# w_gu with four rows of a partition side by side, loaded by halves of an expert

## The chip, the cores and the metric

The kernel runs on one core of a Trainium2 chip. The metric is the device time of one execution in microseconds. Before the change the median of three runs is 1074.6 us (1073.11 to 1078.62).

## The reference

One decoder layer on 256 tokens of width 1024, all in float32. A state-space mixer (S5 with a GLU) and a cross-attention into 256 memory rows read one input projection; their outputs are joined by w_out, added to the input and normalized. What the change touches is the mixture of experts that follows:

```python
logits = xt @ router_w + router_b
top_val, top_idx = lax.top_k(logits, 4)          # of 32 experts
gates = softmax(top_val)
# for every expert e, on the tokens that chose it:
gu = xb @ w_gu[e] + b_gu[e]                      # 1024 -> 2048
x_glu = minimum(gu[..., :1024], 7.0)
x_lin = clip(gu[..., 1024:], -7.0, 7.0)
act = x_glu * sigmoid(1.702 * x_glu) * (x_lin + 1.0)
y = act @ w_down[e] + b_down[e]                  # 1024 -> 1024
out = sum over the chosen experts of gate * y
```

followed by a second residual and layer norm. Each expert's w_gu is 1024 x 2048 floats (8 MB) and its w_down 1024 x 1024 (4 MB); the 32 experts together are 402.7 million bytes, and every one is read once.

## The kernel before, in words

SBUF holds one tile `big` of 23 slots; a slot is 2048 floats on each of 128 partitions, 1 MB. The mixer's phase (until about 143 us) keeps its tensors in these slots under names (`slot_of`, L85 to L92; `big_tile`, L94). Slots 0 to 21 form eleven blocks of two neighbouring slots, 2 MB each, and they are also the ring through which the experts' weights stream: `ring` (L99) holds the blocks' first slots in the order in which the mixer's phase lets go of them, and `next_block` (L101) takes the first and puts it behind the last.

`load_gu` (L1183) issues four loads for an expert's w_gu, one for each block. A load has 256 rows of w_gu, two to a partition: partition p gets rows 2p and 2p + 1, which lie next to each other in HBM, so each partition's part is one run of 16 KB. `load_down` (L1192) issues two loads for w_down, four rows of 4 KB to a partition, also runs of 16 KB. The loads are issued on SyncE (SP), whose instructions are kept in the order in which they are written (`Ordered`, L127). A load waits, on SyncE, until the matmuls that read the block's former content are done; later loads stand behind it. Six loads make an expert. At e = 18 one block leaves the ring for b_down and the last norm's rows (L1302 to L1307), and ten remain.

On TensorE, expert after expert: `up` (L1113) multiplies the expert's gathered tokens (64 slots, transposed) with w_gu in eight steps of 128 rows; `act` runs on VectorE and ScalarE; meanwhile TensorE gathers the tokens of the next two experts (`gather_pair`, L1084, at odd e) or adds the finished pair of experts into the output's accumulators (`combine`, L1159, at even e); then `act_t` transposes the activations, `up_bias` starts the next expert's sums with its bias, and `down` (L1145) multiplies with w_down. A step of 128 rows of w_gu takes every second row of a load (row t * 256 + 2 * r + j for step 2t + j), so the gather picks the columns of h_sb in the same order through `hv` (L1058), with a step of two floats between neighbouring columns.

The last two experts are arranged by hand (L1309 to L1348): expert 31's w_gu is loaded before expert 30's w_down, and expert 31's w_down in smaller cuts. A branch for experts with more than 64 tokens (L1382 on) uses the same functions; the times below are without it.

Of the kernel before, what the change touches and what calls it, by code (L numbers as in the profile page):

```python
# [16 lines left out]
P = 128  # L17
D = 1024
NT = 256
KT = D // P  # L20
# [3 lines left out]
NE = 32  # L24
# [2 lines left out]
LN_EPS = 1e-5  # L27
MISS = 8192.0
ROWS = 2
NBIG = 23  # L30

LOG2E = 1.4426950408889634
# [9 lines left out]
def kernel(  # L42
# [32 lines left out]
    V, S, PE, G, SP = nc.vector, nc.scalar, nc.tensor, nc.gpsimd, nc.sync  # L75

    keep = ctx.enter_context(tc.tile_pool(name="keep", bufs=1))
    big = ctx.enter_context(tc.tile_pool(name="big", bufs=1)).tile([P, NBIG * 2048], F32, tag="big", name="big")
    psum = ctx.enter_context(tc.tile_pool(name="psum", bufs=8, space=bass.MemoryType.PSUM))
# [2 lines left out]
    prep = pre.enter_context(tc.tile_pool(name="pre", bufs=1))  # L82


    slot_of = {}  # L85
    for k, names in enumerate((
# [3 lines left out]
    )):  # L90
        for name in names.split():
            slot_of[name] = k  # L92

    def big_tile(name):  # L94
        k = slot_of[name]
        return big[:, 2048 * k : 2048 * (k + 1)]


    ring = [2 * k + n for k in (0, 1, 2, 3, 4, 8, 6, 10, 7, 9, 5) for n in range(0, 2, ROWS)]  # L99

    def next_block():  # L101
        ring.append(ring.pop(0))
        return big[:, 2048 * ring[-1] : 2048 * (ring[-1] + ROWS)]

    def bank(name):
        return psum.tile([P, 512], F32, tag="ps", name=name)
# [32 lines left out]
    SP = Ordered(SP)  # L139

    def mm(o, lhsT, rhs, start, stop, shared=False):
        pin(PE.matmul(o, lhsT, rhs, start=start, stop=stop, skip_group_check=shared))  # L142
# [7 lines left out]
    def ts(o, x0, s1, op0, s2=None, op1=ALU.bypass, eng=None):  # L150
        return (eng or V).tensor_scalar(out=o, in0=x0, scalar1=s1, scalar2=s2, op0=op0, op1=op1)
# [34 lines left out]
    for k2 in range(4):  # L186
        t = big_tile(f"win_{k2}").rearrange("p (k n) -> p k n", k=2)
        rows = w_in[2 * k2 * P : (2 * k2 + 2) * P, :].rearrange("(k p) n -> p k n", p=P)
# [390 lines left out]
    for b in range(3):  # L579
        ps = bank(f"kb{b}")  # L580
# [59 lines left out]
    for b in range(3):  # L640
        for a in range(2):
            ps = bank(f"kc{b}{a}")
# [66 lines left out]
    for r2 in range(3):  # L709
        ps = bank(f"sip{r2}")  # L710
# [14 lines left out]
    for q in range(2):  # L725
        dst = sv[q].rearrange("p (j l c) -> p l j c", j=4, l=6)
        for l0, l1 in ((0, 4), (4, 6)):
            ps = bank(f"stp{q}{l0}")
# [62 lines left out]
    for i in range(2):  # L791
        for m in range(2):
            ps = bank(f"pTp{i}{m}")
# [71 lines left out]
    for t4 in range(2):  # L865
        ts_ = slice(4 * t4, 4 * t4 + 4)
        ps = bank(f"yTa{t4}")
# [3 lines left out]
    for t4 in range(2):  # L871
        ts_ = slice(4 * t4, 4 * t4 + 4)
        ps = bank(f"yTb{t4}")
# [10 lines left out]
    for mq in range(6):  # L884
        ps = bank(f"zp{mq}")
# [45 lines left out]
    h_sb = big_tile("h_sb").rearrange("p (i d) -> p i d", i=2)  # L931
# [21 lines left out]
    def wt(shape, tag, name, dt=F32):  # L953
        n = 2 if tag == "ogT" else 1
        return work.tile(list(shape), dt, tag=tag, name=f"{tag}_{name}", bufs=n)
# [54 lines left out]
    def up_bias(n, sel, ps=None):  # L1010

        ps = [bank(f"gu{b}_{n}") for b in range(2)] if ps is None else ps
        for hf in range(2):
            for b in range(2):
                mm(
                    ps[b][64 * hf : 64 * hf + 64, :], sel[2 * b + hf],
                    bgu[NE * (2 * b + hf) : NE * (2 * b + hf) + NE, :], True, False, True,
                )
        return ps

    def sel_of(e):
        return [ident[NE * q : NE * q + NE, NE * q + e : NE * q + e + 1].to_broadcast([NE, CAP]) for q in range(4)]
# [25 lines left out]
    ps = up_bias("e0", sel_of(0))  # L1048
# [6 lines left out]

    dbg("@experts", None)

    hv = h_sb.rearrange("p i (t r j) -> p i t j r", r=P, j=ROWS)  # L1058

    def gather(n, xg, ranks, base, between=lambda: None, after=lambda: None, oh=None):  # L1060

        w = CAP * len(ranks)
        first_too = oh is None
        oh = wt((P, 2, 2 * CAP), "oh", n) if oh is None else oh
        ps = [bank(f"xgp{k}_{n}") for k in range(len(ranks))]
        for i in range(2):
            if i:
                between()
            for k, rank in enumerate(ranks):
                if i or first_too:  # L1070
                    ts(oh[:, i, CAP * k : CAP * k + CAP], base, rank[i], ALU.is_equal)
            if i:
                after()
            for kt in range(KT):
                c = w * kt % 512
                mm(
                    ps[w * kt // 512][:, c : c + w], hv[:, i, kt // ROWS, kt % ROWS], oh[:, i, 0:w],
                    c == 0 and i == 0, i == 1, True,
                )
        k = 512 // w  # L1080
        for n_, p in enumerate(ps):
            S.copy(xg[:, k * n_ : k * n_ + k, :], p.rearrange("p (k c) -> p k c", k=k))

    def gather_pair(n, xg, ranks):  # L1084

        oh = wt((P, 2, 2 * CAP), "oh", n)
        for i in range(2):
            for k, rank in enumerate(ranks):
                ts(oh[:, i, CAP * k : CAP * k + CAP], iota64, rank[i], ALU.is_equal)
        for k4 in range(2):  # L1090
            ps = bank(f"xgp{k4}_{n}")
            for i in range(2):
                for kt in range(4 * k4, 4 * k4 + 4):
                    mm(
                        ps[:, P * (kt % 4) : P * (kt % 4) + P], hv[:, i, kt // ROWS, kt % ROWS], oh[:, i, :],
                        kt % 4 == 0 and i == 0, i == 1, True,
                    )
            S.copy(xg[:, 4 * k4 : 4 * k4 + 4, :], ps.rearrange("p (k c) -> p k c", k=4))
# [36 lines left out]
    def act_t(n, a, ps=None, at=None):  # L1135
        ps = bank(f"atp_{n}") if ps is None else ps
        av = a.rearrange("s (c p j) -> s c j p", p=P, j=2 * ROWS)
        for c in range(4):
# [41 lines left out]
                mm(ps, ogT[:, i, :], y[:, ds_], True, True)  # L1180
                tt(acc[:, i, ds_], acc[:, i, ds_], ps, ALU.add)

    def load_gu(src):  # L1183

        w = []
        for t in range(KT // ROWS):
            b = next_block().rearrange("p (j n) -> p j n", j=ROWS)
            SP.dma_start(b, src[t * ROWS * P : (t + 1) * ROWS * P, :].rearrange("(p j) n -> p j n", j=ROWS))
            w += [b[:, j, :] for j in range(ROWS)]
        return w  # L1190

    def load_down(src, split=False):  # L1192
# [50 lines left out]
    def load_gb2(n):  # L1243
        return padded("rows2", D, ((slice(0, 1), ln2_g), (slice(1, 2), ln2_b)))
# [56 lines left out]
    for e in range(NE):  # L1301
        if e == NE - 14:  # L1302
            k = ring[0]
            slot_of.update(bd=k, gb2=k, rows2=k + 1, o=k + 1)
            del ring[0 : 2 // ROWS]
            late = padded("bd", D + NT, ((slice(0, NE), b_down[0]),))
            rows2 = load_gb2("e")  # L1307
        gu = load_gu(w_gu[0, e]) if e < NE - 1 else gu_last
        if e == NE - 2:  # L1309
            gu_last = load_gu(w_gu[0, e + 1])  # L1310
        if e != NE - 2:
# [20 lines left out]
        if e == NE - 2:  # L1332
# [6 lines left out]
            ps = up_bias(f"e{e + 1}", sel_of(e + 1), tb[1:3])  # L1339
# [26 lines left out]
        ps = up_bias(f"e{e + 1}", sel_of(e + 1))  # L1366
# [15 lines left out]
    with tc.If(fullest > CAP):  # L1382
# [6 lines left out]
        with tc.For_i(0, NE, 1) as e:  # L1389
# [10 lines left out]
            for rnd in range(1, NT // CAP):  # L1400
# [10 lines left out]
                ps = up_bias(f"f{rnd}", sel)  # L1411
                gu = load_gu(gsrc)
# [45 lines left out]
```

## Time and profile before

| | |
|---|---|
| median of 3 runs | 1074.6 us (1073.11 to 1078.62) |
| the profiled execution's own time | 1072.42 us |
| its span, first to last instruction | 1070.6 us |
| TensorE matmul busy | 1003.3 us, 94% |
| mean granted TensorE clock | 0.995 |
| bytes moved by DMA | 424.61 MB, 397 GB/s over the span |

The profile is that of one execution. PE is TensorE, PEld its weight loads, DVE is VectorE, ACT ScalarE, POOL GpSimd, and SPq the instructions of SyncE's sequencer, among them the issues of loads. A matmul's end is modelled, so a busy TensorE is not one at its peak. Most instructions carry the line of a helper (L142 is `mm`, L145 `tr`, L135 the ordered engines); they are told apart by the names of what they write and read.

### The profile page before, as it was taken

How to read it: one execution, taken by the hardware profiler on the slowest of the kernel's cores; microseconds unless marked ns; L12 is line 12 of the kernel's file. 1: busy time of each engine (PE TensorE's matmuls, PEld its weight loads, DVE VectorE, ACT ScalarE, POOL GpSimd, SP SyncE). 2: the span in 40 equal slices, each digit the busy share in tenths (PEclk: the TensorE clock that was granted, in tenths of full speed). 3: DMA queues.
4: the chain of work that ended last, by engine and by line, in shares of the span. 5: the costliest groups of instructions: out<-in, count | busy, mean ns of one | idle time of the engine just before them, and what ended most of it. 6: DMA issues, size and time to landing. Idle time of an engine off the chain costs nothing.

```text
span 1070.6 us, 12357 instructions
## 1 busy us (share of the span) xinstructions
PE 1003.3 (94%) x5297; PEld 442.6 (41%) x5297; DVE 245.6 (23%) x531; ACT 150.4 (14%) x288; POOL 49.2 (5%) x90
## 2 busy tenths in 40 slices
PE   9999999999999999999999988899999999898994
PEld 8886554434343434343434332323333343333331
DVE  7984251111111111111111111110111111111113
ACT  3494020101010101010101000000101110100001
POOL 5810000000000000000000000000000000000001
PEclk9999999999999999999999999999999999999998
DMA  9949989999999999999999999999999999999992
GB/s 303 166 151 329 424 314 429 428 417 430 427 428 427 425 429 428 426 430 427 428 426 429 429 409 428 429 428 427 427 427 428 427 428 427 427 428 428 429 422 98
DMA packets 43939, 424.61 MB, mean 397 GB/s; under 512 B 11251, under 2 KB 14215, under 8 KB 19177
## 3 DMA queue, kind: packets, MB, share of 16 engines
q1 hardware_dynamic: 43384, 422.73, 95.9%
q10 hardware_dynamic: 496, 1.05, 0.3%
q8 instruction: 43, 0.70, 0.3%
q14 instruction: 16, 0.12, 0.0%
HBM read 421.93 MB, written 1.84 MB: 396 GB/s over the span
## 4 chain that ended last, share of the span: by engine, by line
PE 50%; DMA 45%; DVE 2%; ACT 1%; issue 0%; SPq 0%; ACTq 0%; POOL 0%; DVEq 0%; POOLq 0%
DMA big<-in_exp_w_gu_dram 29%; PE gu_e L142 20%; PE dn_e L142 11%; DMA big<-in_exp_w_down_dram 11%; PE xgp_e L142 4%; DMA big<-in_exp_b_down_dram 4%; PE accp L142 3%; PE yp L142 3%; DVE big L135 2%; PE ups L142 1%; PE zp L142 1%; DMA big<-in_l_w_in_dram 1%; PE tail L142 1%; ACT big L135 1%; PE atp_e L145 1%; PE qps L142 1%
## 5 line engine op out<-in xcount | busy, mean ns | idle before, releaser
L142 PE MATMUL gu_e<-big,xg_e 128*64 128x512 f32 x1984 | 439.8, 594 | 44.2 <-DMA big<-in_exp_w_gu_dram 43.5
L142 PEld LDWEIGHTS gu_e<-big,xg_e 128*64 128x64 f32 x1984 | 138.3, 137 | 340.0 <-issue 253.0
L142 PE MATMUL dn_e<-big,xl_te 128*64 128x512 f32 x960 | 212.6, 595 | 0.0
L142 PEld LDWEIGHTS dn_e<-big,xl_te 128*64 128x64 f32 x960 | 66.3, 137 | 144.3 <-issue 119.6
L1127 DVE TENSOR_SCALAR xl_e<-gu_e 128x512 f32<-128x512 f32 x31 | 21.4, 691 | 429.2 <-PE gu_e L142 429.2
L1155 DVE COPY y_e<-dn_e 64x512 f32<-64x512 f32 x30 | 20.5, 684 | 265.7 <-PE dn_e L142 265.7
L135 ACT ACTIVATE gu_e<-xl_e 128x512 f32<-128x512 f32 x31 | 18.6, 601 | 403.7 <-DVE xl_e L1127 403.7
L142 PEld LDWEIGHTS xgp_e<-oh_e,big 128*128 128x128 f32 x544 | 65.4, 196 | 13.3 <-PE gu_e L142 12.2
L142 PE MATMUL xgp_e<-oh_e,big 128*128 128x128 f32 (+1 forms) x544 | 68.7, 284 | 0.0
L142 PE MATMUL accp<-y_e,ogT_e 128*128 128x512 f32 x128 | 59.4, 603 | 0.8 <-DVE y_e L1155 0.8
L135 ACT COPY y_e<-dn_e 64x512 f32<-64x512 f32 x30 | 17.5, 582 | 244.0 <-DVE y_e L1155 244.0
L142 PEld LDWEIGHTS accp<-y_e,ogT_e 128*128 128x128 f32 x128 | 23.2, 190 | 35.3 <-issue 33.7
L142 PE MATMUL gu_e<-bgu,ident 32*64 32x512 f32 x248 | 34.3, 612 | 0.0
L135 DVE TENSOR_TENSOR big<-big 128x96 f32<-128x96 f32 (+8 forms) x47 | 29.0, 635 | 21.1 <-ACT big L135 16.2
L142 PE MATMUL yp<-big 128*128 128x512 f32 x64 | 28.6, 596 | 0.0
L135 DVE TENSOR_TENSOR big<-big,tab 128x2048 f32<-128x2048 f32 x12 | 26.5, 2276 | 0.2 <-DVE big L135 0.2
L135 ACT COPY xl_te<-atp_e 128x512 f32<-128x512 f32 x30 | 17.9, 595 | 60.4 <-PE atp_e L145 57.5
L135 ACT COPY xg_e<-xgp_e 128x512 f32<-128x512 f32 x32 | 18.8, 587 | 53.4 <-PE xgp_e L142 53.4
L1131 DVE TENSOR_TENSOR xr_e<-xr_e,gu_e 128x512 f32<-128x512 f32 x31 | 21.3, 687 | 6.4 <-ACT gu_e L135 3.3
L135 POOL TENSOR_TENSOR yv<-yv,mhalf 128x1 f32<-128x1 f32 x2 | 1.1, 550 | 468.9 <-DVE yv L135 468.9
L1238 POOL MEMSET big<- 128x1280 f32 (+1 forms) x2 | 2.1, 1058 | 447.0 <-PE gu_e L142 447.0
L1130 DVE SCALAR_TENSOR_TENSOR xr_e<-xr_e,xl_e 128x512 f32<-128x512 f32 x32 | 22.1, 692 | 1.1
(289 smaller groups left out, 586.7 us busy)
## 6 DMA issues: line engine op xcount, KB each, us to landing
big<-in_exp_w_gu_dram SPq DMA_DIRECT2D x128, 2048.0 KB, 39.1
big<-in_exp_w_down_dram SPq DMA_DIRECT2D x62, 2048.0 KB, 33.8
big<-in_l_w_in_dram SPq DMA_DIRECT2D x3, 1024.0 KB
big<-in_w_out_dram SPq DMA_DIRECT2D x3, 1024.0 KB, 9.2
big<-in_exp_w_down_dram SPq DMA_DIRECT2D x3, 1024.0 KB
big<-in_x_dram SPq DMA_DIRECT2D x3, 512.0 KB, 3.5
big<-in_l_s_w_glu_dram SPq DMA_DIRECT2D x2, 768.0 KB
big<-in_l_w_in_dram SPq DMA_DIRECT2D x2, 512.0 KB, 6.8
```

The costliest lines, as they stand in the source:

```text
L135: return lambda *a, **k: pin(f(*a, **k))
L142: pin(PE.matmul(o, lhsT, rhs, start=start, stop=stop, skip_group_check=shared))
L145: pin(PE.transpose(o, in_, ident if idn is None else idn))
L1127: V.tensor_scalar(out=xl_, in0=ps[0], scalar1=7.0, scalar2=None, op0=ALU.min)
L1130: V.scalar_tensor_tensor(out=xr, in0=xr, scalar=1.0, in1=xl_, op0=ALU.add, op1=ALU.mult)
L1131: a = V.tensor_tensor(out=xr, in0=xr, in1=sg, op=ALU.mult)
L1155: eng(y[:, 512 * dh : 512 * dh + 512], ps[dh][64 * dh : 64 * dh + 64, :])
L1238: G.memset(t[:, 0:width], 0.0)
```

## The change

The slots are renumbered so that the ring's order is 0, 2, 4 up to 20: a name that stood in block b now stands in the block at b's place in the old order. `load_gu` takes 512 rows at a time, four to a partition, so that a partition's part is one run of 32 KB over two blocks. For experts 3 to 28, and where the two blocks are neighbours in memory, both are filled by one load of 4 MB; otherwise each block is filled by a load of its own, with the first or the second 16 KB of each run. The steps of `up` and the gather follow with `GJ = 4`: step 4t + j takes row t * 512 + 4 * r + j, and neighbouring columns of h_sb are four floats apart.

```diff
--- before.py
+++ after.py
@@ -27,6 +27,7 @@
 LN_EPS = 1e-5
 MISS = 8192.0
 ROWS = 2
+GJ = 4
 NBIG = 23
 
 LOG2E = 1.4426950408889634
@@ -82,6 +83,7 @@
     prep = pre.enter_context(tc.tile_pool(name="pre", bufs=1))
 
 
+    free_order = (0, 1, 2, 3, 4, 8, 6, 10, 7, 9, 5)
     slot_of = {}
     for k, names in enumerate((
         "ptmp0 wsc", "ptmp1 gt", "m20", "m21", "m22", "u_sb", "cab s_in tw yg", "memT xs", "bbt tz0", "bab att",
@@ -89,14 +91,14 @@
         "win_3 wgl0", "win_0 sv wo2", "win_1 tz2 ymT", "wk wgl1", "pow yT", "wv h_sb",
     )):
         for name in names.split():
-            slot_of[name] = k
+            slot_of[name] = 2 * free_order.index(k // 2) + k % 2 if k < 22 else k
 
     def big_tile(name):
         k = slot_of[name]
         return big[:, 2048 * k : 2048 * (k + 1)]
 
 
-    ring = [2 * k + n for k in (0, 1, 2, 3, 4, 8, 6, 10, 7, 9, 5) for n in range(0, 2, ROWS)]
+    ring = list(range(0, 22, ROWS))
 
     def next_block():
         ring.append(ring.pop(0))
@@ -1055,7 +1057,7 @@
 
     dbg("@experts", None)
 
-    hv = h_sb.rearrange("p i (t r j) -> p i t j r", r=P, j=ROWS)
+    hv = h_sb.rearrange("p i (t r j) -> p i t j r", r=P, j=GJ)
 
     def gather(n, xg, ranks, base, between=lambda: None, after=lambda: None, oh=None):
 
@@ -1074,7 +1076,7 @@
             for kt in range(KT):
                 c = w * kt % 512
                 mm(
-                    ps[w * kt // 512][:, c : c + w], hv[:, i, kt // ROWS, kt % ROWS], oh[:, i, 0:w],
+                    ps[w * kt // 512][:, c : c + w], hv[:, i, kt // GJ, kt % GJ], oh[:, i, 0:w],
                     c == 0 and i == 0, i == 1, True,
                 )
         k = 512 // w
@@ -1092,7 +1094,7 @@
             for i in range(2):
                 for kt in range(4 * k4, 4 * k4 + 4):
                     mm(
-                        ps[:, P * (kt % 4) : P * (kt % 4) + P], hv[:, i, kt // ROWS, kt % ROWS], oh[:, i, :],
+                        ps[:, P * (kt % 4) : P * (kt % 4) + P], hv[:, i, kt // GJ, kt % GJ], oh[:, i, :],
                         kt % 4 == 0 and i == 0, i == 1, True,
                     )
             S.copy(xg[:, 4 * k4 : 4 * k4 + 4, :], ps.rearrange("p (k c) -> p k c", k=4))
@@ -1180,13 +1182,22 @@
                 mm(ps, ogT[:, i, :], y[:, ds_], True, True)
                 tt(acc[:, i, ds_], acc[:, i, ds_], ps, ALU.add)
 
-    def load_gu(src):
+    def load_gu(src, whole=False):
 
         w = []
-        for t in range(KT // ROWS):
-            b = next_block().rearrange("p (j n) -> p j n", j=ROWS)
-            SP.dma_start(b, src[t * ROWS * P : (t + 1) * ROWS * P, :].rearrange("(p j) n -> p j n", j=ROWS))
-            w += [b[:, j, :] for j in range(ROWS)]
+        for t in range(KT // GJ):
+            rows = src[t * GJ * P : (t + 1) * GJ * P, :].rearrange("(p j) n -> p j n", j=GJ)
+            next_block(), next_block()
+            k0, k1 = ring[-2:]
+            if whole and k1 == k0 + ROWS:
+                b = big[:, 2048 * k0 : 2048 * (k0 + GJ)].rearrange("p (j n) -> p j n", j=GJ)
+                SP.dma_start(b, rows)
+                w += [b[:, j, :] for j in range(GJ)]
+                continue
+            for n, k in enumerate((k0, k1)):
+                b = big[:, 2048 * k : 2048 * (k + ROWS)].rearrange("p (j n) -> p j n", j=ROWS)
+                SP.dma_start(b, rows[:, ROWS * n : ROWS * n + ROWS])
+                w += [b[:, j, :] for j in range(ROWS)]
         return w
 
     def load_down(src, split=False):
@@ -1305,7 +1316,7 @@
             del ring[0 : 2 // ROWS]
             late = padded("bd", D + NT, ((slice(0, NE), b_down[0]),))
             rows2 = load_gb2("e")
-        gu = load_gu(w_gu[0, e]) if e < NE - 1 else gu_last
+        gu = load_gu(w_gu[0, e], 3 <= e < NE - 3) if e < NE - 1 else gu_last
         if e == NE - 2:
             gu_last = load_gu(w_gu[0, e + 1])
         if e != NE - 2:
```

## Rows read from the trace of the kernel before

**Rows 1.** The page's second part: 40 equal slices of the span, busy tenths, then GB/s.

```profile
PE   9999999999999999999999988899999999898994
...
DMA  9949989999999999999999999999999999999992
GB/s 303 166 151 329 424 314 429 428 417 430 427 428 427 425 429 428 426 430 427 428 426 429 429 409 428 429 428 427 427 427 428 427 428 427 427 428 428 429 422 98
```

**Rows 2.** Chain of waits: start us, us, what; two experts, then the hops.

```profile
255.83 7.02 PE dn_e L142 x32
...
281.69 7.08 PE dn_e L142 x32
...
308.22 7.02 PE dn_e L142 x32
...
484.44 39.09 DMA big<-in_exp_w_gu_dram
...
1002.92 39.09 DMA big<-in_exp_w_down_dram
```

**Rows 3.** Windows: stretch, length, busy us (x instructions) by engine, PEclk, DMA share, GB/s.

```profile
135.80:139.00 3.20, 3.20 (x11) 1.69 (x11) 2.42 (x10) 0.00 (x0) 0.00 (x0) 1.00 0.00 0
139.00:229.60 90.60, 87.18 (x456) 40.20 (x456) 22.54 (x62) 11.45 (x21) 0.55 (x1) 0.98 1.00 417
229.60:234.60 5.00, 5.00 (x26) 1.69 (x24) 0.00 (x0) 0.00 (x0) 0.00 (x0) 1.00 1.04 416
234.60:240.00 5.40, 5.40 (x28) 1.75 (x26) 0.68 (x1) 0.58 (x1) 0.00 (x0) 1.00 0.94 388
240.00:440.00 200.00, 200.00 (x990) 79.55 (x988) 33.42 (x71) 18.98 (x35) 0.00 (x0) 1.00 1.01 428
```

**Rows 4.** The same view over stretches with 1 KB and 4 KB runs.

```profile
34.00:38.00 4.00, 4.00 (x25) 3.64 (x24) 4.00 (x3) 2.49 (x5) 4.00 (x2) 1.00 1.04 366
76.00:80.00 4.00, 4.00 (x51) 3.36 (x53) 3.93 (x7) 3.92 (x10) 0.19 (x1) 1.00 1.01 393
78.00:80.00 2.00, 2.00 (x42) 1.59 (x44) 1.93 (x3) 1.94 (x4) 0.19 (x1) 1.00 1.03 412
```

**Rows 5.** SyncE's timeline: start us, us from first to last, queue, line, what, xcount.

```profile
138.06 0.33 SPq L135 DMA_DIRECT2D big<-in_exp_w_gu_dram  x1
...
183.33 3.76 SPq L135 DMA_DIRECT2D big<-in_exp_w_gu_dram  x2
...
199.46 0.33 SPq L135 DMA_DIRECT2D big<-in_exp_w_gu_dram  x1
...
209.76 3.76 SPq L135 DMA_DIRECT2D big<-in_exp_w_gu_dram  x2
...
216.63 0.33 SPq L135 DMA_DIRECT2D big<-in_exp_w_gu_dram  x1
...
232.98 0.33 SPq L135 DMA_DIRECT2D big<-in_exp_w_gu_dram  x1
...
236.41 3.76 SPq L135 DMA_DIRECT2D big<-in_exp_w_down_dram  x2
...
285.38 0.33 SPq L135 DMA_DIRECT2D big<-in_exp_w_gu_dram  x1
```

**Rows 6.** TensorE's timeline; in brackets the idle time before, and its cause.

```profile
219.04 5.40 PE L142 MATMUL accp<-big,xl_alpha 128*128 128x512 f32 x8 [2.45 <-DVE xl_alpha L1163]
...
229.28 7.09 PE L142 MATMUL dn_e<-big,xl_te 128*64 128x512 f32 x32
...
622.96 3.65 PE L142 MATMUL gu_e<-big,xg_e 128*64 128x512 f32 x16 [2.76 <-DMA big<-in_exp_w_gu_dram]
627.86 2.37 PE L142 MATMUL gu_e<-big,xg_e 128*64 128x512 f32 x10 [1.25 <-DMA big<-in_exp_w_gu_dram]
```

**Rows 7.** TensorE's weight loads, 240 to 440 us: xcount, busy us, mean ns, idle before.

```profile
L142 PEld LDWEIGHTS xgp_e<-oh_e,big 128*128 128x128 f32 x128 | 15.4, 196 | 3.2 <-PE gu_e L142 3.2
...
L145 PEld LDWEIGHTS atp_e<-ident,xr_e 128*128 128x128 f32 x32 | 4.8, 205 | 1.9 <-issue 1.9
```

## The prediction

> **What bounds the kernel now.** I read the busy shares by slice first, then the chain of waits, the windows by stage, and SyncE's own timeline. The slices show TensorE and the DMA engines both near full, so neither is the bound by its share alone [rows 1]. The chain separates them in time: until about 446 us it runs through TensorE, expert after expert, and after that it jumps from one weight load to the next in hops of 39.09 us down to the last at 1002.92, which lands at 1042.01; a short tail on TensorE follows [rows 2]. Two consecutive experts take 308.22 - 255.83 = 52.39 us of TensorE, 26.2 us each. A hop of 39.09 us is eight loads (SyncE issues a load when the eighth before it has landed), 4.89 us for 2 MB, so six loads of an expert take 29.3 us. TensorE is therefore 3.1 us per expert faster than the queue. It starts with a full ring, eats that lead up by 446 us, and from then on follows the queue.
>
> So the end is set by the DMA queue over the whole stretch from 139 us on. Nothing moves from 135.8 to 139.0; after that the engines' share stays at 1.0, from 240 us on with 428 GB/s, and only at 234.6 to 240.0 does it dip, to 0.94 and 388 GB/s [rows 1, 3]. Any microsecond in which the queue has nothing to do between 139 and 1040 us, early or late, arrives at the end whole; any gain in rate does too, as long as TensorE keeps some of its 3.1 us. That dip is the place to look at: the queue was all but empty there.
>
> **The change, part by part.** Numbering loads from 0, six per expert, load n goes into the block of load n - 11 until expert 18, where the ring drops to ten blocks.
>
> *The number of whole pairs.* Between e = 3 and 28 there are 26 x 2 = 52 pairs. A pair that straddles the ring's end stays two loads: e = 5, 9, 16 (one each) with eleven blocks, e = 18, 21, 23, 26, 28 with ten. 44 become one load of 4 MB.
>
> *Longer contiguous runs.* A load is 128 runs, eight per DMA engine. The trace has no 32 KB run, so I take the cost of a run from the rates: 16 KB runs at 428 GB/s take 16384 / (428/16) = 612.5 ns on an engine; the 4 KB runs of w_out, at 412 GB/s from 78 to 80 us, take 159.1 ns [rows 4]. That is (612.5 - 159.1) / 12288 = 0.0369 ns a byte, and 159.1 - 4096 x 0.0369 = 8.0 ns are left as a constant of each run. A whole pair has eight runs fewer on each engine: 8 x 8.0 = 64 ns, 0.064 us. The wider window at 393 GB/s, which takes in loads of smaller runs, would give 18 ns a run and 0.146 us; the 1 KB runs at 366 GB/s give 6.9 ns [rows 4]. The lower end is zero: a long run may still be moved in 16 KB pieces. I take 0.064 us, since 4 KB is the nearest clean row: over 40 pairs -2.6 us, ends 0 and -5.8. (40, not 44: what the first four pairs save only lengthens the stall below.)
> The Trainium skill, "DMA: Bandwidth & Descriptors", section "Why small descriptors are slow (HBM only)", speaks of a fixed overhead of some 3 cycles a packet, with beats of 32 bytes. By that rule two 16 KB runs are 1030 beats and one 32 KB run 1027, an estimate of 0.029 us a pair and -1.1 us in all, which would make the sum +3.4 instead of +1.9; the rows show a larger constant, and I go by them.
>
> *The wait that is added.* A whole pair may be issued only when both of its blocks are free, that is when its second load was issued before. While TensorE sets the pace, a load is issued the moment its block is read out: 3.43 us apart inside w_gu, with a break of 9 to 16 us where combine, transposes and bias lie. Going through the early pairs against the queue [rows 3, 5]: 139.0 to 229.6 us at 417 GB/s is 37.8 MB, exactly the 18 loads 8 to 25, so load 25 is done at about 229.6.
> - Expert 3, loads 18/19: issue 186.76 instead of 183.33 (the row's 3.76 us less the 0.33 of one issue); load 17 ends at about 190.3, covered. Loads 20/21: 199.46 for both, where the first of them went out 9 us earlier; load 19 ends at about 200.1, and with the cold start below the queue loses about 1 us, which the next item swallows.
> - Expert 4, loads 24/25: 213.19 instead of 209.76, with the queue busy to about 220; covered. Loads 26/27: before, 26 was issued at 216.63, and its transfer (229.6 to 234.6) is what kept the queue alive until 27 was issued at 232.98. Now neither goes out before 232.98, when TensorE is halfway through the w_down matmuls of expert 2 (229.28 to 236.37 [rows 6]). The queue is dry from about 230.
> - What a cold start costs: the load issued at 138.06 moves its first byte at 139.0, 0.95 us later; and load 27, issued at 232.98, was done at 240.0, 7.0 us for 4.89 us of data, 2.1 us [rows 3, 5]. With 1.8 us as the value, the pair is done at 232.98 + 1.8 + 9.7 = 244.5 instead of 240.0: +4.5 us; with 0.95 +3.6, with 2.1 +4.8.
> Behind the waiting load on SyncE stand the w_down loads of expert 4, which were issued at 236.41 anyway because their blocks come free then; they lose nothing more. For expert 6, loads 38/39 wait to 285.38, while the queue, now 4.5 us late, is busy with loads 28 to 37 until 244.5 + 10 x 4.89 = 293.4. From there the margin grows by 3.1 us an expert; after 446 us the ring's eleven blocks are 54 us of queue time (ten: 49), a load is read out within some 20 us of landing, and a pair is free about 30 us before its turn. One stall, then.
>
> *Halves of an expert for TensorE.* Before 446 us it works on data that landed long ago. After that it waits for 4 MB where it waited for 2 MB: two waits of about 1.25 us per expert [rows 6] become one of about 3 us. The total is the 3.1 us that it has to spare, so this costs nothing; a wait of 2.76 us at 622.96 left the clock alone, while 2.45 us at 219.04 preceded the one stretch at half clock, which the windows show as 0.98 up to 229.6 [rows 3, 6]. Should each long wait cost such a drop, TensorE would have some 1.7 us more per expert and still fit. The last three experts are loaded as before, so the tail is what it was.
>
> *The rest at nothing.* The gather reads h_sb at a step of four floats instead of two: its weight loads take 196 ns on average, the transposes that already step by four 205 ns [rows 7], at most 9 ns x 64 before 232.98, +0.6 us. Renumbering moves tiles within `big` and leaves the order of reuse as it was. Half as many load issues on SyncE: 0.33 us each, hidden behind a 39 us backlog. The halves of experts 0 to 2, 29 to 31 and of split pairs have 16 KB runs as now, 32 KB apart.
>
> **Sum.** +4.5 - 2.6 = +1.9 us, ends -2.2 (3.6 - 5.8) and +5.4 (4.8 + 0.6, nothing saved). On the profiled execution's own 1072.42 us (span 1070.6 and 1.8 around it) that is 1074.3. The median of the runs shown stands 2.2 us above that execution, so I predict 1074.6 + 1.9 = 1076.5 us.
>
> **Rivals.**
> - *No stall, only the shorter transfers.* If the queue is restarted in the shadow of bytes still under way, or the blocks come free sooner, 44 pairs at 0.064 give 1074.6 - 2.8 = 1071.8, and at 0.146 1068.2. The rows for the dip at 234.6 speak against it: with load 26 in front, load 27 came just too late.
> - *The runs stay 16 KB inside the engines.* Then only the stall is left: 1074.6 + 4.5 = 1079.1. The steady constant from 1 KB to 16 KB speaks for a cost per run, but nothing shows a longer run.
> - *Slower: rows 32 KB apart are read more slowly.* Every w_gu load changes its reach: an engine's neighbours start twice as far apart in HBM. Place: all w_gu loads from expert 3 on, 29 x 19.6 = 568 us of queue time, so each per cent of rate is 5.7 us; from 0.6% on it carries my +1.9 past half a per cent of the kernel (5.4 us), and at 2% it gives 1076.5 + 11.4 = 1087.9. Against it: w_out with 4 KB rows and w_gu with 16 KB rows lie on one line of cost per byte. The Trainium skill, same page, section "Latency and other measured facts", tells of copies that slow down with a large power-of-two row pitch: 207 GB/s of 214 at 512 KiB, 103 at 4 MiB. By that rule 32 KB would lie well below where the loss begins, and the case would give 1076.5 again; no row here has a pitch above 16 KB, so the case keeps its chance.
>
> **How the numbers follow.** Forecast 0.62, no stall 0.14, runs stay short 0.12, slower reads 0.12. A difference under 0.5% (5.4 us: 1069.2 to 1080.0) can't be told from none. Faster: half of the no-stall case and a little of the forecast, 0.08. Slower: most of the slow reads and a share of the third and the first, 0.16. Within: 0.76. The range runs from the middle of the no-stall case, 1070, to the stall with no saving and the spread of the runs (1073.1 to 1078.6) on top, 1082.
>
> **What would show it.** Right: the page lists some 44 loads of 4096 KB; a window with almost no bytes between 230 and 235 us; then a rate a little above 428 GB/s, 430 or so. Wrong: no empty window near 232 (the stall), a rate still at 427 to 428 (the runs), a rate below it (slow reads), or SyncE waiting for TensorE after 446 us with the engines' share below 1.0, which would mean that the ring, not the queue, sets the pace.

## The result, and the profile after

The changed kernel takes 1087.14 us (median of 4 runs, 1085.90 to 1090.71) against 1074.56 us of the kernel before in the same comparison (4 runs, 1073.11 to 1078.62): a ratio of 1.0128, 95% interval 1.0106 to 1.0151. That is 12.6 us slower, where 1.9 us and no difference that can be told were forecast. The profiled execution is the longest of the four, 1090.71 us with a span of 1089.0.

The page of the changed kernel: granted clock and GB/s in 40 slices, the sums of the chain, the whole pairs (count, size, median us from issue to landing), and the gather's weight loads from the costliest groups.

```profile
PEclk9999968999999999999999999999999999999998
...
GB/s 298 173 128 327 425 235 318 377 385 394 426 429 428 431 430 433 430 428 431 427 431 429 427 423 416 430 431 428 435 429 429 429 430 431 421 429 429 426 423 115
...
PE 89%; DMA 7%; DVE 2%; ACT 1%; issue 0%; ACTq 0%; POOL 0%; DVEq 0%; POOLq 0%
...
L144 PEld LDWEIGHTS xgp_e<-oh_e,big 128*128 128x128 f32 x544 | 128.3, 329 | 13.7 <-PE gu_e L144 12.2
...
big<-in_exp_w_gu_dram SPq DMA_DIRECT2D x44, 4096.0 KB, 31.4
```

The 44 whole pairs are there. Against [rows 1], slices 6 to 10 (136 to 272 us) move 235 to 394 GB/s where they moved 314 to 430; from slice 11 on the rate is about as before, in most slices a little above it. The clock's row, which on the page of before has a 9 in every slice but the last, has a 6 and an 8 in slices 6 and 7. So the time went between 136 and 252 us, in a stretch where the forecast had the queue covered but for one dip. On the costliest list the gather has changed: its weight loads take 329 ns where [rows 7] has 196, and its matmuls grow with them (the row is shown further down).

TensorE's timeline of the changed kernel, first three gathers (start us, us from first to last, instructions; in brackets the idle time before):

```profile
147.05 4.00 PE L144 MATMUL xgp_e<-oh_e,big 128*128 128x64 f32 x16
...
152.23 3.81 PE L144 MATMUL xgp_e<-oh_e,big 128*128 128x64 f32 x16
156.77 16.89 PE L144 MATMUL gu_e<-big,xg_e 128*64 128x512 f32 x64 [0.73 <-ACT xg_e L137]
...
173.80 7.73 PE L144 MATMUL xgp_e<-oh_e,big 128*128 128x64 f32 x32
...
184.23 8.25 PE L144 MATMUL dn_e<-big,xl_te 128*64 128x512 f32 x32
...
206.14 7.73 PE L144 MATMUL xgp_e<-oh_e,big 128*128 128x128 f32 x32
```

The same stretch of the kernel before:

```profile
149.80 13.95 PE L142 MATMUL gu_e<-big,xg_e 128*64 128x512 f32 x64 [0.73 <-ACT xg_e L135]
163.89 3.98 PE L142 MATMUL xgp_e<-oh_e,big 128*128 128x64 f32 x32
...
169.33 7.09 PE L142 MATMUL dn_e<-big,xl_te 128*64 128x512 f32 x32
```

A gather of 32 matmuls takes 7.73 us instead of 3.98. The two matmul groups behind slow gathers took longer as well, 16.89 for 13.95 us and 8.25 for 7.09, though the change does not touch them. The w_down matmuls of expert 0 start at 184.23 instead of 169.33, 14.9 us late. Of that 2.3 us are older than any gather: in this execution the router's first matmuls begin at 136.59 instead of 134.32. (Among the profiled executions of both layouts this start lies anywhere between 134.32 and 136.59.) The gathers give 7.4 us (4.00 + 3.81 against twice 2.10 for the first, 7.73 against 3.98 for the second). Most of the rest goes with two stretches at half clock, which the windows show (columns as in [rows 3]); first the changed kernel:

```profile
130.00:252.00 122.00, 118.62 (x520) 60.06 (x520) 29.93 (x80) 12.64 (x23) 1.61 (x2) 0.89 0.81 332
145.60:162.80 17.20, 16.47 (x62) 10.56 (x56) 6.33 (x26) 3.64 (x7) 0.00 (x0) 0.50 0.70 275
159.90:164.30 4.40, 4.40 (x16) 1.27 (x14) 1.04 (x5) 0.00 (x0) 0.00 (x0) 0.68 0.00 0
176.40:186.60 10.20, 10.20 (x40) 6.65 (x42) 0.74 (x4) 1.17 (x2) 0.00 (x0) 0.50 0.82 349
186.30:189.90 3.60, 3.60 (x18) 1.12 (x16) 0.00 (x0) 0.00 (x0) 0.00 (x0) 0.96 0.00 0
216.70:220.10 3.40, 3.40 (x18) 1.15 (x16) 0.00 (x0) 0.00 (x0) 0.00 (x0) 1.00 0.00 0
252.00:1000.00 748.00, 746.11 (x3422) 323.40 (x3420) 111.54 (x235) 66.62 (x123) 2.05 (x2) 1.00 1.00 428
```

and the kernel before:

```profile
130.00:252.00 122.00, 118.58 (x605) 54.29 (x604) 32.55 (x84) 13.80 (x25) 1.62 (x2) 0.99 0.96 400
...
252.00:1000.00 748.00, 706.94 (x3440) 273.36 (x3440) 112.38 (x240) 68.02 (x126) 2.05 (x2) 1.00 1.01 427
```

SyncE's timeline of the changed kernel at the three stretches with 0 GB/s:

```profile
163.41 0.33 SPq L137 DMA_DIRECT2D big<-in_exp_w_down_dram  x1
...
189.09 0.33 SPq L137 DMA_DIRECT2D big<-in_exp_w_gu_dram  x1
...
219.21 0.33 SPq L137 DMA_DIRECT2D big<-in_exp_w_gu_dram  x1
```

The reader is to see three things. The queue stands still three times, at 159.9, 186.3 and 216.7: each time SyncE issues the next load only at 163.41, 189.09 and 219.21, and of the 125 us that it waits between 130 and 252 us, 115 are for TensorE's matmuls, those that still read the blocks above all. From 145.6 to 162.8 and from 176.4 to 186.6 the granted clock is 0.50, that is 1.2 of 2.4 GHz; the second stretch begins 2.6 us into a slow gather, the first 1.4 us before one. And between 130 and 252 us the kernel moves (400 - 332) GB/s x 122 us = 8.3 MB less than before, 19.4 us of queue time at 428 GB/s, while from 252 to 1000 us it moves 1 GB/s more (320.40 MB against 319.37, 2.4 us). The difference, 17.0 us, and the 2.3 us of the late start are about what separates the two profiled executions (1090.71 - 1072.42 = 18.3). From 252 us on TensorE is busy for 746.11 of 748 us, and the chain follows it for 89% of the span; yet the DMA engines are full there too, as before. Which of them sets the end is not told by the chain; a run below decides it (`late32`).

### The profile page after: what moved, and what is told of

Its sections match the earlier page's. It is cut to its first block, busy times and chain, and to the rows that moved or that the text cites. A ratio compares the mean times of both kernels' runs of the same rounds, so it can differ in the third digit from the quotient of the medians.

```text
span 1089.0 us, 12257 instructions
## 1 busy us (share of the span) xinstructions
PE 1064.4 (98%) x5297; PEld 512.7 (47%) x5297; DVE 245.8 (23%) x531; ACT 150.4 (14%) x288; POOL 49.2 (5%) x90
## 4 chain that ended last, share of the span: by engine, by line
PE 89%; DMA 7%; DVE 2%; ACT 1%; issue 0%; ACTq 0%; POOL 0%; DVEq 0%; POOLq 0%
PE gu_e L144 39%; PE dn_e L144 19%; PE xgp_e L144 12%; PE accp L144 5%; DMA big<-in_exp_w_down_dram 4%; DMA big<-in_exp_w_gu_dram 3%; PE yp L144 3%; PE ups L144 2%; DVE big L137 2%; PE zp L144 1%; PE atp_e L147 1%; ACT big L137 1%; PE tail L144 1%; PE qps L144 1%; PE busy L144 1%; PE kb L144 0%
## 5 line engine op out<-in xcount | busy, mean ns | idle before, releaser
L144 PE MATMUL gu_e<-big,xg_e 128*64 128x512 f32 x1984 | 434.2, 595 | 2.6 <-DMA big<-in_exp_w_gu_dram 1.9
L144 PEld LDWEIGHTS gu_e<-big,xg_e 128*64 128x64 f32 x1984 | 142.8, 138 | 288.2 <-issue 283.1
L144 PEld LDWEIGHTS xgp_e<-oh_e,big 128*128 128x128 f32 x544 | 128.3, 329 | 13.7 <-PE gu_e L144 12.2
L144 PE MATMUL xgp_e<-oh_e,big 128*128 128x128 f32 (+1 forms) x544 | 131.5, 404 | 0.0
L153 DVE TENSOR_SCALAR oh_e<-iota,rk 128x64 f32<-128x64 f32 x62 | 12.8, 252 | 85.2 <-PE xgp_e L144 85.2
```

## The experiments

Nine kernels ran. A text on record calls the kernel before B and the changed one A. The ratios are to the kernel before in the same comparison, as recorded with it; they are not the quotients of the medians (1087.14 / 1074.56 is 1.0117 for the changed kernel, where the ratio is 1.0128). Losses in microseconds are differences of medians.

**Which part of the change costs.** Theory S: the gather's step of four floats (TensorE's weight loads) costs it. Theory P: the whole pairs, their waits or their 32 KB runs, do.

`a_step2`: the changed kernel with the gather's step of before, in both gather functions.
```
-    hv = h_sb.rearrange("p i (t r j) -> p i t j r", r=P, j=GJ)
+    hv = h_sb.rearrange("p i (t r j) -> p i t j r", r=P, j=ROWS)
...
-                    ps[w * kt // 512][:, c : c + w], hv[:, i, kt // GJ, kt % GJ], oh[:, i, 0:w],
+                    ps[w * kt // 512][:, c : c + w], hv[:, i, kt // ROWS, kt % ROWS], oh[:, i, 0:w],
```


> The changed kernel, with the gather reading h_sb at a step of two floats again (it then gathers other columns than the weights' rows, so only the times count). Theory S (the step of the gather): its 544 weight loads take 196 ns and follow each other every 118 ns again, TensorE gets 62.8 us back, the queue's early dry stretches of 4.5, 3.8 and 3.6 us at 160, 186 and 217 us are gone but for the one that whole pairs bring at expert 4, and the time is 1076 us (1073 to 1079). Theory P (the whole pairs' wait and the 32 KB runs): nothing changes in them, 1087 us.

Measured 1071.94 us against 1073.96, ratio 0.9982 (0.9964 to 1.0000): all of the loss is gone, and the median is 2.0 us below the kernel before, with an interval that reaches 1. The gather's weight loads in its groups (count, busy us, mean ns, idle before):

```profile
L144 PEld LDWEIGHTS xgp_e<-oh_e,big 128*128 128x128 f32 x544 | 65.5, 196 | 13.3 <-PE gu_e L144 12.2 <-DVE m L137 0.8 <-DVE oh_e L137 0.2
```

and its windows:

```profile
130.00:252.00 122.00, 118.58 (x615) 54.88 (x613) 32.94 (x84) 14.39 (x26) 1.62 (x2) 1.00 0.94 391
...
230.00:240.00 10.00, 10.00 (x48) 3.30 (x46) 0.68 (x1) 0.58 (x1) 0.00 (x0) 1.00 0.80 318
252.00:1000.00 748.00, 713.98 (x3435) 277.68 (x3435) 112.49 (x239) 67.59 (x126) 2.05 (x2) 0.98 1.00 429
```

`b_step4`: the kernel before with the changed kernel's step and nothing else.
```
-    hv = h_sb.rearrange("p i (t r j) -> p i t j r", r=P, j=ROWS)
+    hv = h_sb.rearrange("p i (t r j) -> p i t j r", r=P, j=4)
...
-                    ps[w * kt // 512][:, c : c + w], hv[:, i, kt // ROWS, kt % ROWS], oh[:, i, 0:w],
+                    ps[w * kt // 512][:, c : c + w], hv[:, i, kt // 4, kt % 4], oh[:, i, 0:w],
```


> The kernel before, with the gather reading h_sb at a step of four floats and nothing else changed (other columns are gathered, only the times count). Theory S: weight loads of 329 ns, 62.8 us more on TensorE, half-clock stretches between 145 and 190 us, the queue dry early, 1083 to 1088 us. Theory P: 1074.6 us, as before, with TensorE's spare time taking the longer gather.

Measured 1086.31 us, ratio 1.0136 (1.0106 to 1.0166), +12.4 us: one edit of an access pattern, no load touched, gives the whole loss. The two parts add up to 10.4 us beside the 12.6 measured, inside their intervals. S stands; P is out. Its windows show a kernel whose queue runs short early only:

```profile
130.00:252.00 122.00, 118.58 (x536) 60.18 (x536) 30.41 (x81) 12.71 (x24) 1.61 (x2) 0.94 0.88 357
...
252.00:1000.00 748.00, 747.30 (x3430) 323.76 (x3428) 110.83 (x234) 66.59 (x123) 2.05 (x2) 1.00 1.01 427
```

`a_perm`: the changed kernel with h_sb kept in the gather's order, so that the weight loads read neighbouring floats; the norm's two VectorE operations and the combine's matmul permute instead.
```
-    h_sb = big_tile("h_sb").rearrange("p (i d) -> p i d", i=2)
+    h_sb = big_tile("h_sb").rearrange("p (i t j r) -> p i t j r", i=2, j=GJ, r=P)
+
+    def by_step(half):
+        return half.rearrange("p (r j) -> p j r", j=GJ)
...
-        stt(h_sb[:, i, hs], x2[:, i, hs], mean[i], gb[:, 0, hs], ALU.subtract, ALU.mult)
+        stt(h_sb[:, i, hf], by_step(x2[:, i, hs]), mean[i], by_step(gb[:, 0, hs]), ALU.subtract, ALU.mult)
...
-        stt(h_sb[:, i, hs], h_sb[:, i, hs], rs[i], gb[:, 1, hs], ALU.mult, ALU.add)
+        stt(h_sb[:, i, hf], h_sb[:, i, hf], rs[i], by_step(gb[:, 1, hs]), ALU.mult, ALU.add)
...
-    hv = h_sb.rearrange("p i (t r j) -> p i t j r", r=P, j=GJ)
+    hv = h_sb
...
-                    mm(accp[i][hf], alpha_id, h_sb[:, i, 512 * hf : 512 * hf + 512], True, False)
+                    mm(by_step(accp[i][hf]), alpha_id, h_sb[:, i, hf], True, False)
```


> The changed kernel with h_sb stored in the order of the steps, so that the gather's weight loads read 128 neighbouring floats; the norm writes it in that order, and the first matmuls into the accumulators write their sums back in the natural one. Theory S: weight loads of 190 ns, every 118 ns or a little less, and 1073 to 1077 us; if the norm's strided reads cost VectorE something just before the first expert, up to 3 us more. Theory P: 1087 us.

Measured 1076.24 us, ratio 1.0037 (1.0021 to 1.0054), +2.3 us, and 4.3 above `a_step2`, from which only the gather, the norm and the combine's first matmuls differ. The weight loads are cured, but the norm became slower in turn. Its gather's weight loads, in the groups:

```profile
L144 PEld LDWEIGHTS xgp_e<-oh_e,big 128*128 128x128 f32 x544 | 62.6, 193 | 13.8 <-PE gu_e L144 12.2 <-DVE big L137 0.8 <-DVE oh_e L137 0.7
```

VectorE's timeline at the norm (start us, us, instructions):

```profile
132.85 2.20 DVE L137 SCALAR_TENSOR_TENSOR big<-big,mv 128x512 f32<-128x512 f32 x2
```

the same two operations of the kernel before:

```profile
132.03 1.41 DVE L135 SCALAR_TENSOR_TENSOR big<-big,mv 128x512 f32<-128x512 f32 x2
```

and two windows of `a_perm` behind them:

```profile
150.40:157.20 6.80, 6.07 (x19) 2.47 (x19) 2.70 (x11) 3.64 (x7) 0.00 (x0) 0.50 0.85 313
157.60:159.40 1.80, 1.80 (x10) 0.56 (x8) 0.00 (x0) 0.00 (x0) 0.00 (x0) 1.00 0.04 9
```

Reading two inputs at a step of four floats costs VectorE 1.10 us an operation instead of 0.70. The router's matmuls begin as in `a_step2` (135.14 and 135.16), but the matmuls with w_gu behind the first gather start 1.7 us later (152.31 and 150.65); then the clock is down for 6.8 us and the queue all but dry for 1.8. The strided read was moved to another engine and paid there; why the clock fell is not shown.

`b_step8`: the step at eight floats, to see whether the price grows with the bytes passed over.
```
-    hv = h_sb.rearrange("p i (t r j) -> p i t j r", r=P, j=ROWS)
+    hv = h_sb.rearrange("p i (t r j) -> p i t j r", r=P, j=8)
...
-                    ps[w * kt // 512][:, c : c + w], hv[:, i, kt // ROWS, kt % ROWS], oh[:, i, 0:w],
+                    ps[w * kt // 512][:, c : c + w], hv[:, i, kt // 8, kt % 8], oh[:, i, 0:w],
...
```


> The kernel before with the gather at a step of eight floats (other columns, only the times count). If a weight load costs by the bytes that its columns span, 466 ns from one to the next, 190 us more on TensorE, which is then the bound: about 1190 us. If it costs by the number of separate reads, which a step of four already has at its worst, 233 ns as at a step of four and 1083 to 1088 us.

```profile
L142 PEld LDWEIGHTS xgp_e<-oh_e,big 128*128 128x128 f32 x544 | 130.9, 334 | 13.6 <-PE gu_e L142 12.2 <-DVE m L135 0.8 <-DVE big L135 0.5
```

334 ns and 1088.62 us in a single run. The price is full at four floats and does not grow with the bytes passed over.

**Where TensorE's time counts.** The slow weight loads cost TensorE 3.75 us a gather, 64 us over the 17 gathers of 32, and the kernel 12.4. Theory Q: a slow gather costs only while the queue has no lead (few loads wait in it), up to some 250 us. Theory R: a share of every gather's cost arrives.

`late32`: experts 6 to 29 loaded and gathered as in the changed kernel, the others as before.
```
+    def rows_of(e):
+        return GJ if 6 <= e < NE - 2 else ROWS
...
-        gu = load_gu(w_gu[0, e], 3 <= e < NE - 3) if e < NE - 1 else gu_last
+        gu = load_gu(w_gu[0, e], rows_of(e)) if e < NE - 1 else gu_last
```


> Same result as the reference's. Experts 6 to 29 are loaded and gathered as in the changed kernel (32 KB runs, whole pairs where the ring allows, step of four floats in the gather), experts 0 to 5 and 30, 31 as in the kernel before. 41 whole pairs; 12 gathers with slow weight loads, 12 x 32 x 0.116 = 44.5 us more on TensorE. Theory Q (a slow gather costs only while the queue has no lead, before some 250 us): those 44.5 us are hidden, no stall at expert 4, 41 pairs save 0.064 to 0.093 us each, so 2.6 to 3.8 us below the kernel before: about 1071 us. Theory R (each slow gather costs its share of the 12.4 us lost with all 17): 384 of 544 weight loads, +8.7 us, less the saving, 1079 us.

Measured 1071.19 us against 1072.85, ratio 0.9982 (0.9962 to 1.0003). Its late window:

```profile
252.00:1000.00 748.00, 743.60 (x3436) 322.47 (x3436) 114.19 (x242) 68.57 (x127) 2.05 (x2) 1.00 1.00 429
```

TensorE is busy 36.7 us longer than before between 252 and 1000 us, 743.60 of 748, and the kernel loses nothing. That answers what the chain left open: with TensorE nearly as full as in the changed kernel, the late stretch still runs at the queue's rate.

`b_early4`: the kernel before with the step of four in the first three gathers alone (experts 0, 1 and the pair 2/3).
```
-    hv = h_sb.rearrange("p i (t r j) -> p i t j r", r=P, j=ROWS)
+    hvs = {j: h_sb.rearrange("p i (t r j) -> p i t j r", r=P, j=j) for j in (2, 4)}
...
+        j = 4 if n in ("e0", "e1") else 2
...
+        j = 4 if n == "e2" else 2
...
+                    ps[w * kt // 512][:, c : c + w], hvs[j][:, i, kt // j, kt % j], oh[:, i, 0:w],
```


> The kernel before with a step of four floats in the first three gathers alone (experts 0, 1 and the pair 2 and 3; other columns there, only the times count), 96 of the 544 weight loads, 11.1 us more on TensorE. Theory Q: nearly the whole loss of all slow gathers, 1083 to 1086 us, with the queue dry near 158 and 183 us. Theory R: 96 of 544 of 12.4 us, 1076 us.

Measured 1085.03 us, ratio 1.0118 (1.0102 to 1.0134): +12.2 us from three gathers, nearly all that seventeen cost. TensorE's timeline at the w_down matmuls of expert 2, behind all three gathers ([rows 6] has them at 229.28), and the windows:

```profile
242.89 7.09 PE L142 MATMUL dn_e<-big,xl_te 128*64 128x512 f32 x32
```

```profile
130.00:252.00 122.00, 118.62 (x537) 60.35 (x537) 30.16 (x80) 13.23 (x24) 1.61 (x2) 0.93 0.87 352
145.00:190.00 45.00, 44.27 (x190) 24.64 (x191) 9.17 (x28) 6.00 (x11) 0.00 (x0) 0.81 0.79 312
```

Q stands and R is out.

`a_step2_halves`: as `a_step2`, but no whole pair; each load keeps 16 KB runs, 32 KB apart.
```
-        gu = load_gu(w_gu[0, e], 3 <= e < NE - 3) if e < NE - 1 else gu_last
+        gu = load_gu(w_gu[0, e]) if e < NE - 1 else gu_last
```


> The changed kernel with the gather at a step of two floats (other columns, only the times count) and no whole pair: every w_gu load is 2 MB, 16 KB runs that lie 32 KB apart. If the rest of the change is only the wait at expert 4 and the saving of the longer runs, both are gone and the time is that of the kernel before, 1073 to 1075 us. If 16 KB runs at a pitch of 32 KB are read more slowly, each per cent adds some 5.7 us.

Measured 1073.32 us, ratio 1.0007 (0.9993 to 1.0022), with 427 GB/s from 252 to 1000 us as before:

```profile
230.00:240.00 10.00, 10.00 (x52) 3.38 (x53) 0.68 (x1) 1.17 (x2) 0.00 (x0) 1.00 1.00 413
252.00:1000.00 748.00, 709.47 (x3450) 275.83 (x3450) 114.02 (x242) 68.61 (x127) 2.05 (x2) 1.00 1.01 427
```

So the wider pitch costs nothing, the dip at 230 us in `a_step2` (0.80, 318 GB/s) comes from the whole pairs, and so does the higher rate later.

**What the early time consists of.** Three gathers are 96 weight loads at 0.116 us more, 11.1 us, and `b_early4` lost 12.2. Theory T: any TensorE time spent early is lost whole, whatever spends it. Theory U: slow weight loads do something of their own.

`b_fill`: the kernel before with 42 filler matmuls (84 instructions) put into the same three gathers, at the fast step: seven in each half of the first two, seven in each group of four steps of the pair's.
```
+            if n in ("e0", "e1"):
+                busy(7)
...
+            if n == "e2":
+                busy(7)
```


> The kernel before, with its fast gathers, and 42 matmuls of ones with ones, 128 x 128, put into the first three gathers where the slow weight loads lengthened them: 14 in expert 0's, 14 in expert 1's, 14 in that of the pair 2 and 3, about 3.7 us each, 11.1 us of TensorE as in b_early4, without a slow weight load. Theory T (any time that TensorE loses this early is lost to the queue): the clock may stay at full speed, since TensorE multiplies all along; then the 4 us or so that b_early4 also lost at half clock are spared, and the time is 1079 to 1082 us; with half-clock stretches as there, 1085 us. Theory U (the slow weight loads do it in another way than by their time, such as by slowing the DMA's writes into the same memory): 1073 us.

Measured 1081.27 us against 1072.78, ratio 1.0077 (1.0060 to 1.0094), +8.5 us. TensorE's timeline at the router's first matmuls, at one group of fillers and at the w_down matmuls of expert 2, and the windows:

```profile
136.40 1.92 PE L142 MATMUL lgp<-wg,xg_hT 128*128 128x32 f32 x16
...
148.12 1.78 PE L142 MATMUL busy<-ones 128*128 128x128 f32 x14
...
240.07 7.09 PE L142 MATMUL dn_e<-big,xl_te 128*64 128x512 f32 x32
```

```profile
130.00:252.00 122.00, 119.22 (x638) 59.84 (x638) 30.55 (x81) 13.41 (x24) 1.61 (x2) 0.99 0.90 370
145.00:190.00 45.00, 44.96 (x279) 24.86 (x280) 10.99 (x36) 5.99 (x11) 0.00 (x0) 1.00 0.93 372
```

The w_down matmuls of expert 2 start at 240.07 instead of 229.28, 10.8 us late. Of that 2.1 us are older than any gather (the router begins at 136.40 instead of 134.32), so the six groups of fillers delay TensorE by 8.7 us: less than the 11.1 intended, since they overlap with their neighbours and fill some of its idle time. The kernel lost 8.5 us. T holds: TensorE time spent early arrives almost whole, whatever spends it.

In `b_early4` the router begins on time (134.32), and the same matmuls start at 242.89, 13.6 us late, for 12.2 us lost. So the fillers are no equal of its slow loads. They delay TensorE 4.9 us less; about half of that is the shorter length (8.7 us against 11.1), and the rest goes with the clock, which stays at 1.00 between 145 and 190 us where `b_early4` has 0.81. (A short half-clock stretch at the combine near 232 us, in `b_fill` as in the kernel before and not in `b_early4`, takes some of that back.) The losses differ by 3.7 us (their intervals, 10.9 to 14.4 and 6.4 to 10.1 us, do not overlap). U is not needed for them; what is left open is why the clock falls beside the slow loads and not beside the fillers.

`b_step3`: the step at three floats, the last point of the curve; in both gather functions the stationary operand alone changes.
```
-                    ... hv[:, i, kt // ROWS, kt % ROWS], ...
+                    ... h_sb[:, i, 512 * (kt // 4) + kt % 4 : 512 * (kt // 4) + kt % 4 + 3 * P - 2 : 3], ...
```


> The kernel before with all gathers at a step of three floats (other columns, only the times count). A weight load takes 196 ns at a step of one or two and 329 ns at four or eight. If the cost sets in when a step passes 8 bytes, 329 ns and 1086 us; if at 16 bytes, 196 ns and 1073 us; a value between says that it grows with the step up to four.

```profile
L142 PEld LDWEIGHTS xgp_e<-oh_e,big 128*128 128x128 f32 x544 | 96.8, 263 | 13.3 <-PE gu_e L142 12.2 <-DVE m L135 0.8 <-DVE oh_e L135 0.2
```

263 ns and 1082.01 us in a single run, halfway between the steps of two and four.

## Why the prediction was wrong, point by point

**The step that failed is "The rest at nothing".** It priced the gather's step of four floats at "at most 9 ns x 64 before 232.98, +0.6 us", from 196 ns for the gather's weight loads and 205 ns for transposes that "already step by four" [rows 7]. These are two kinds of instruction, and the price of a step can't be read between kinds. The row for it was in the trace: the same transposes at a step of one. TensorE's weight loads of the kernel before, 100 to 240 us (count, busy us, mean ns, idle before):

```profile
L142 PEld LDWEIGHTS xgp_e<-oh_e,big 128*128 128x128 f32 x96 | 11.6, 196 | 1.9 <-DVE m L135 0.8 <-PE gu_e L142 0.8 <-DVE oh_e L135 0.2
L145 PEld LDWEIGHTS hTp<-ident,big 128*128 128x128 f32 x16 | 1.9, 141 | 1.9 <-issue 1.3 <-DVE big L135 0.3 <-DVE msk L135 0.2
L145 PEld LDWEIGHTS atp_e<-ident,xr_e 128*128 128x128 f32 x12 | 1.8, 210 | 0.5 <-issue 0.5
```

Transposes at a step of one take 141 ns, at four 210. Against its own kind a step of four costs 69 ns there; the gather paid 133 (329 - 196), and the sum had no upper end for it. The count was short as well: 96 weight loads lie before 232.98, not 64. At the transposes' 69 ns they are an estimate of 6.6 us, from rows that I had; at the 0.116 us that a gather's matmul really took more (131.5 us of busy TensorE for 544 against 68.7 before, 62.8 / 544) they are 11.1 us. Either would have put the forecast on the slower side:

```profile
L144 PE MATMUL xgp_e<-oh_e,big 128*128 128x128 f32 (+1 forms) x544 | 131.5, 404 | 0.0
```

**The queue sets the end: right, and it says what early time costs.** The prediction held that any microsecond in which the queue is idle between 139 and 1040 us arrives at the end. The bytes that a profiled execution moves less than the one of before between 130 and 252 us (400 GB/s there), turned into time at 428 GB/s, come within some 2 us of how much longer it is than 1072.42: `b_fill` 30 x 122 / 428 = 8.6 us (1081.66, 9.2 longer), `b_early4` 13.7 (1085.06, 12.6), `b_step4` 12.3 (1086.77, 14.4); in `b_fill` and `b_step4` the router also began 2.1 us late. What the prediction did not draw from it is that TensorE's pace has little slack before 250 us. It had the lead as "a full ring", but the loads through expert 4 are issued when a block is read out, with little left in the queue: its own walk through the pairs left 3.5 us at loads 18/19 (190.3 - 186.76) and some 7 at 24/25. So most of a delay of TensorE becomes a delay of the queue: 8.5 of 8.7 us in `b_fill`, 12.2 of 13.6 in `b_early4`.

**The wait of whole pairs: there, and smaller, in part by luck.** The forecast had the pair of expert 4 go out at 232.98, the queue dry from about 230, and 4.5 us lost. SyncE's timeline of `a_step2`, and TensorE's at the combine before it:

```profile
232.13 0.33 SPq L137 DMA_DIRECT2D big<-in_exp_w_gu_dram  x1
...
219.88 3.70 PE L144 MATMUL accp<-big,xl_alpha 128*128 128x512 f32 x8 [2.45 <-DVE xl_alpha L1165]
```

and three of its windows there:

```profile
231.00:232.00 1.00, 1.00 (x8) 0.37 (x6) 0.00 (x0) 0.00 (x0) 0.00 (x0) 1.00 0.23 98
232.00:233.00 1.00, 1.00 (x8) 0.35 (x6) 0.00 (x0) 0.00 (x0) 0.00 (x0) 1.00 0.00 0
233.00:234.00 1.00, 1.00 (x6) 0.29 (x4) 0.00 (x0) 0.00 (x0) 0.00 (x0) 1.00 1.71 459
```

The empty window is there, but short: the queue runs out in the microsecond from 231, later than 230, and moves again at 233, 0.9 us after the issue; the sum took 1.8 for a cold start. From 130 to 252 us the kernel moves 391 GB/s against 400, 9 x 122 / 428 = 2.6 us, and that includes what loads 20 and 21 lost earlier. Part of the difference from 4.5 is luck: the pair went out 0.85 us sooner than forecast although this execution's router began 0.84 us later (135.16 against 134.32), since the combine's eight matmuls took 3.70 us where [rows 6] has 5.40. The half-clock stretch of the kernel before was not there, and with it the queue would have stood up to 1.7 us longer (an estimate, 5.40 - 3.70).

**Longer runs: right in kind, a little larger.** From 252 to 1000 us `a_step2` moves 320.67 MB where the kernel before moves 319.37, 3.0 us at 428 GB/s; the sum had 2.6 and its upper end 5.8. The two terms come to -0.4 us by these windows, and to -2.0 (-3.9 to 0) by the medians, instead of +1.9. The Trainium skill, "DMA: Bandwidth & Descriptors", section "Why small descriptors are slow (HBM only)", gave an estimate of 1.1 us; the trace shows 3.0.

**Halves for TensorE at nothing: right.** In `a_step2` the clock fell to 0.98 between 252 and 1000 us, as the long waits could have made it, and TensorE's 713.98 us still fit.

**The rivals.** The stall was smaller than forecast but not absent; the runs do not stay at 16 KB, since the kernels that show 429 all have whole pairs and the one without shows 427; and rows 32 KB apart are not read more slowly, since `a_step2_halves` keeps 427. The rival that happened, TensorE slower at its weight loads, was not among them. All signs that the prediction named lie in the DMA's rows and SyncE's waits; the largest change was in a row of TensorE. One of its signs of being wrong came by half: from 446 to 1000 us SyncE waits mostly for TensorE, in the changed kernel (464 us for its two large matmul groups) and in `a_step2` (363), where the kernel before waits for loads to land. But the engines' share does not fall below 1.00 with it, so the queue stays full and sets the pace all the same.

**The best version.** `late32` is 1.7 us below the kernel before, with an interval that reaches 1: not to be told from it.

## What to carry to other kernels

When a layout change makes another engine read with a larger step, price that read like against like: find the same kind of instruction in the trace at both steps, and where there is none, leave the price open or run that one read at both steps. Another kind is no bound: the transposes lost 69 ns at the step that cost the gather 133. Ask of every engine "off the bound" in which stretch the bound still waits for it: here three slow gathers before 250 us, 11 us and the fallen clock beside them, cost 12, and 37 us after that cost none. A layout that pays the queue and taxes TensorE belongs where the queue already has a lead.

## What the runs showed of the hardware

- **Weight loads by step.** A 128x128 f32 weight load took 193 ns at a step of one float (`a_perm`), 196 at two (the kernel before), 263 at three (`b_step3`), 329 at four (the changed kernel) and 334 at eight (`b_step8`). The loss begins past two floats and is complete at four. The Trainium skill, "SBUF — State Buffer", section "Specifications (TRN2)", speaks of lines of 16 bytes of which each should be hit at least twice for full bandwidth: the curve agrees, with four floats to a line, two hits at a step of two and one at four and beyond. The rule speaks against this change, and the prediction did not weigh it.
- **The clock about slow loads.** In all five kernels that gather at three or more floats early (the changed one, `b_step4`, `b_early4`, `b_step8`, `b_step3`) the granted clock is at 1.2 of 2.4 GHz twice between 145 and 190 us. The second stretch begins inside expert 1's slow gather (in `b_early4` the gather starts at 169.86 and the stretch at 174.8). The first begins 3.4 us into expert 0's in `b_early4` and 5.7 us into it in `b_step4`, but ahead of it in the changed kernel. The third slow gather, at 206.14, brings none. Of the kernels with fast early gathers `a_perm` has one such stretch, and the kernel before, `b_fill`, `late32`, `a_step2` and `a_step2_halves` have none there. So the slow loads go with it, and that they alone cause it is not shown.
- **Left open.** Why the clock falls in one of these places and not in another; and the transposes' weight loads rise by only 69 ns at the step that costs the gather 133, which no run explains.
